# Feature-major products of a two-block layer: one 512-column moving operand instead of two of 256, and score products of two heads in turn

## The chip, the cores and the metric

The kernel runs on one core of a Trainium2 chip. The metric is device time in microseconds (us) of one execution. A core has five engines with queues of their own: TensorE (PE, matrix products; its weight loads are listed apart as PEld), VectorE (DVE), ScalarE (ACT), GpSimd (POOL) and SyncE (SP, which here only issues transfers). Each engine works its own list of instructions in order; semaphores tie them together.

## The reference

Two transformer blocks over 256 tokens of width 2048, in float32. Cut to what matters:

```python
# block 1                                    (h = rms_norm(x))
proj = h @ w_in                              # 2048 x 10752: q, k/v, DeltaNet q/k/v, gates
y = merge(nsa_mixer(...) @ w_up_nsa, gated_deltanet(...) @ w_up_dn)   # 1024 x 2048 each
x = x + y @ w_o
x = x + (silu(h2 @ w_ffn_gate) * (h2 @ w_ffn_up)) @ w_ffn_down        # D_FF = 5632
# block 2                                    (h = rms_norm_2(x))
proj = h @ w_in_2                            # RWKV-7 r, k, v, small parts, MLA latents
x = x + concat(rwkv7_mixer(...), mla_mixer(...)) @ w_out_2
gate = causal_conv3(h @ ffn_w_gate_2) + conv_b
x = x + (silu(gate) * (h @ ffn_w_up_2)) @ ffn_w_down_2
```

So nearly all work is matrix products with weights that are read once from memory.

## The kernel before

Float32 exactness is bought with a split: every weight chunk and every activation is written as a high part (fp32r, rounded) and a low part (the rest). A product is three: high x high, high x low, low x high (`mm3`).

Weights come through `wchunks`: SP loads a chunk of 1024 columns per partition (512 KB) into one of five `wraw` buffers, ACT rounds it to `whi` (three buffers), DVE subtracts to `wlo` (three buffers). `wsplit` gives these two instructions priority, so that they stand early in ACT's and DVE's lists.

There are two forms of product. Token-major ones (`gemm_tok`) hold activations as the stationary operand and stream 512 weight columns. Feature-major ones (`gemm_feat`) hold a 128x128 block of weights and stream the activations, 256 tokens. For every block of 128 output features and every k tile of 128 input features they run three products of 256 columns, each with its own weight load; `nm=4` blocks make a product group that fills one of the two `psA` accumulators (4 KB per partition, tile `mmA`). Consumers of a group are `merge_gate` and `merge_up` (gates of the two mixers), `Nsa.first` and `Nsa.q`, `DeltaNet.project` with `conv`, the gate and up loops of both feed-forward layers (FFN), and, with `nm=2`, `Rwkv.project`. A group is read out of the accumulator by one DVE instruction, in `Rwkv.project` by one ACT copy (`padded`).

The activations' parts are separate tiles in numbered slots: `sb`/`sc` and `sd`/`se` hold high and low part of the normed input, `hh`/`hl` that of the second FFN.

Around the mixers, generators are interleaved by `weave`: it always goes on with the first generator whose due time has come, by a table of costs in `Pace`, so that feature-major groups (bulk work) fill the gaps of the dependent chains (attention heads, DeltaNet and RWKV solves, small float32 products in the four `psB` accumulators, tile `pB`). `DeltaNet.project` puts finished groups in `raw` and stops when two are waiting. Outside of `weave` the work stands in program order.

RWKV's `solve` makes for each of four heads two score products (`bt`, `km` against `ar`) that use 64 of the 128 rows; MLA's `scores` makes for each of two heads a full product (`qn`, `kn`), one of 64 rows (`qr`, `kpe`) and a masking product.

Of the kernel before, what the change touches and what calls it, by code (L numbers as in the profile page):

```python
# [18 lines left out]
P = 128  # L19
# [183 lines left out]

class Kern:
    def __init__(self, tc, A, out, ctx):
# [9 lines left out]
        self.cst = None  # L215
        self.later = []

    def slot(self, which, shape, dt=F32):

        return (self.h2 if which in "bc" else self.hpool).tile(shape, dt, name="s" + which, tag="slot_" + which)  # L220
# [323 lines left out]
def hT_tiles(K, slots):  # L544
    return tuple(K.slot(s, [P, KD, T], F32R) for s in slots)


def hidden(K, pool, slots):

    return tuple(Cat(K.slot(s, [P, KD, T], F32R), pool.tile([P, KF - KD, T], F32R, name="hid" + n)) for s, n in zip(slots, "hl"))  # L550


def block1(K, ctx):
# [5 lines left out]
    H = hT_tiles(K, "bc")  # L559
# [22 lines left out]
    with ExitStack() as mix:  # L582
# [27 lines left out]
        M = hT_tiles(K, "bc")  # L610
        run(merge_up(K, dn.odn, A["w_up_dn"][0], td[0], tn, M))
    x = K.slot("a", [P, 2, D])
# [3 lines left out]
    H = hT_tiles(K, "de")  # L616
    run(add_proj(K, x, M, A["w_o"][0], KD, scale=0.5, after=norm_after(K, x, st, "norm2_w", H)))
    r = K.row_scale(st)
    with tc.tile_pool(name="ffn", bufs=1) as fp:
        hid = hidden(K, fp, "bc")  # L620
        for g in range(KF // 4):
            pg = run(K.gemm_feat(H, A["w_ffn_gate"][0], KD, 512 * g))
            if g == 0:
                rb = K.spread(r)
            sg = fp.tile([P, 4, T], F32, name="sg", bufs=2)
            rows4 = rb[:, None, :].to_broadcast([P, 4, T])
            nc.vector.tensor_tensor(sg, pg, rows4, op=ALU.mult)
            nc.scalar.activation(sg, sg, AF.Silu)
            nc.gpsimd.tensor_tensor(sg, sg, rows4, op=ALU.mult)
            pu = run(K.gemm_feat(H, A["w_ffn_up"][0], KD, 512 * g))  # L630
            nc.vector.tensor_tensor(sg, pu, sg, op=ALU.mult)
            K.split(sg, hid[0][:, 4 * g:4 * g + 4], hid[1][:, 4 * g:4 * g + 4])
# [5 lines left out]
        H = hT_tiles(K, "de")  # L638
# [48 lines left out]
def merge_gate(K, H, w_in, rb, half, dst):  # L687

    for g in range(4):
# [43 lines left out]
class DeltaNet:  # L733
# [59 lines left out]
    def conv(self, kind, grp):  # L793

        K, nc, pool = self.K, self.K.nc, self.pool
        while not self.raw:
            yield BLOCK
# [1030 lines left out]
```

## Time and profile before

| | before |
|---|---|
| median of three runs | 2831.42 us (2831.15 to 2832.09) |
| profiled execution | 2832.74 us, its span 2830.8 us |
| PE busy | 2795.0 us (99%), 20080 products |
| PEld busy | 2612.6 us (92%) |
| DVE busy | 1736.4 us (61%) |
| ACT busy | 1267.1 us (45%) |
| POOL busy | 209.8 us (7%) |
| granted TensorE clock | 0.996 of full speed |
| HBM read | 476.30 MB, 170 GB/s over the span |

The span is the time from the first to the last instruction of the profiled execution; 1.9 us of its own time lie around it. Busy shares are averages over very different stretches. The recorded end of a product is modelled and overlaps the next one, so the time that PE spends on one product is read from start to start of neighbours in the list, not from its duration.

### The profile page before, as it was taken

How to read it: one execution, taken by the hardware profiler on the slowest of the kernel's cores; microseconds unless marked ns; L12 is line 12 of the kernel's file. 1: busy time of each engine (PE TensorE's matmuls, PEld its weight loads, DVE VectorE, ACT ScalarE, POOL GpSimd, SP SyncE). 2: the span in 40 equal slices, each digit the busy share in tenths (PEclk: the TensorE clock that was granted, in tenths of full speed). 3: DMA queues.
4: the chain of work that ended last, by engine and by line, in shares of the span. 5: the costliest groups of instructions: out<-in, count | busy, mean ns of one | idle time of the engine just before them, and what ended most of it. 6: DMA issues, size and time to landing. Idle time of an engine off the chain costs nothing. (4 is left out here: it accounts for less than half of the span.)

```text
span 2830.8 us, 48442 instructions
## 1 busy us (share of the span) xinstructions
PE 2795.0 (99%) x20080; PEld 2612.6 (92%) x20080; DVE 1736.4 (61%) x2345; ACT 1267.1 (45%) x1582; POOL 209.8 (7%) x215
## 2 busy tenths in 40 slices
PE   9999999999999999999999999999999999999998
PEld 8997999999899999999888988878899999998888
DVE  6677758855555555555555687786576565655453
ACT  5446445444444444444444554545354444444443
POOL 0000100001000000000000322110000000000000
PEclk9999999999999999999999999999999999999999
DMA  7653366555666666666666653323566666665564
GB/s 234 207 153 115 98 172 180 162 145 183 225 183 180 186 180 186 183 183 188 197 198 186 198 152 98 108 72 123 185 176 181 185 181 184 181 185 189 194 194 138
DMA packets 285565, 484.68 MB, mean 171 GB/s; under 512 B 26113, under 2 KB 77057, under 8 KB 284706
## 3 DMA queue, kind: packets, MB, share of 16 engines
q1 hardware_dynamic: 282688, 475.94, 56.2%
q10 hardware_dynamic: 2658, 5.66, 0.6%
q8 instruction: 157, 2.57, 0.4%
q14 instruction: 62, 0.51, 0.0%
HBM read 476.30 MB, written 5.24 MB: 170 GB/s over the span
## 5 line engine op out<-in xcount | busy, mean ns | idle before, releaser
L257 DVE TENSOR_TENSOR wlo<-wraw,whi 128x1024 fp32r<-128x1024 f32 x889 | 1099.9, 1239 | 853.1 <-ACT whi L256 851.5
L256 ACT CAST whi<-wraw 128x1024 fp32r<-128x1024 f32 x889 | 928.2, 1045 | 1303.7 <-PE mmA L131 1237.6
L131 PE MATMUL mmA<-sd,whi 128*128 128x256 f32 x2256 | 605.4, 286 | 3.2 <-ACT sd L131 1.5
L131 PE MATMUL mmA<-sd,wlo 128*128 128x256 f32 x2048 | 582.1, 284 | 3.4 <-DVE wlo L257 3.4
L131 PE MATMUL mmA<-se,whi 128*128 128x256 f32 x2096 | 568.0, 284 | 0.0
L131 PEld LDWEIGHTS mmA<-sd,whi 128*128 128x128 f32 x2256 | 420.3, 193 | 5.3 <-ACT sd L131 1.7
L131 PE MATMUL mmA<-hh,whi 128*128 128x256 f32 x1408 | 398.7, 283 | 0.0
L131 PEld LDWEIGHTS mmA<-sd,wlo 128*128 128x128 f32 x2048 | 394.1, 192 | 4.9 <-DVE wlo L257 3.8
L131 PE MATMUL mmA<-hh,wlo 128*128 128x256 f32 x1408 | 398.5, 283 | 0.0
L131 PE MATMUL mmA<-hl,whi 128*128 128x256 f32 x1408 | 398.5, 283 | 0.0
L131 PEld LDWEIGHTS mmA<-se,whi 128*128 128x128 f32 x2096 | 393.6, 192 | 0.9 <-issue 0.7
L131 PE MATMUL mmA<-sb,whi 128*128 128x256 f32 x1152 | 331.8, 288 | 1.5 <-ACT whi L256 1.5
L131 PE MATMUL mmA<-sb,wlo 128*128 128x256 f32 x1152 | 328.2, 285 | 1.9 <-DVE wlo L257 1.9
L131 PE MATMUL mmA<-sc,whi 128*128 128x256 f32 x1152 | 327.7, 284 | 0.0
L131 PEld LDWEIGHTS mmA<-hl,whi 128*128 128x128 f32 x1408 | 270.3, 192 | 0.0
L131 PEld LDWEIGHTS mmA<-hh,whi 128*128 128x128 f32 x1408 | 270.3, 192 | 0.0
L131 PEld LDWEIGHTS mmA<-hh,wlo 128*128 128x128 f32 x1408 | 270.3, 192 | 0.0
L131 PEld LDWEIGHTS mmA<-sb,whi 128*128 128x128 f32 x1152 | 221.9, 193 | 3.0 <-ACT whi L256 1.7
L131 PEld LDWEIGHTS mmA<-sb,wlo 128*128 128x128 f32 x1152 | 221.9, 193 | 2.7 <-DVE wlo L257 2.3
L131 PEld LDWEIGHTS mmA<-sc,whi 128*128 128x128 f32 x1152 | 221.8, 193 | 0.9 <-issue 0.7
L131 PE MATMUL mmA<-whi,hidh 128*128 128x512 f32 (+1 forms) x504 | 184.2, 365 | 0.0
L131 PE MATMUL mmA<-wlo,hidh 128*128 128x512 f32 (+1 forms) x504 | 184.2, 365 | 0.0
(418 smaller groups left out, 3749.4 us busy)
## 6 DMA issues: line engine op xcount, KB each, us to landing
wraw<-in_w_in_dram SPq DMA_DIRECT2D x232, 512.0 KB, 3.7
wraw<-in_w_ffn_gate_dram SPq DMA_DIRECT2D x88, 512.0 KB, 3.8
wraw<-in_w_ffn_up_dram SPq DMA_DIRECT2D x88, 512.0 KB, 3.7
wraw<-in_w_ffn_down_dram SPq DMA_DIRECT2D x88, 512.0 KB, 4.7
wraw<-in_ffn_w_gate_dram SPq DMA_DIRECT2D x88, 512.0 KB, 3.7
wraw<-in_ffn_w_up_dram SPq DMA_DIRECT2D x88, 512.0 KB, 3.7
wraw<-in_ffn_w_down_dram SPq DMA_DIRECT2D x88, 512.0 KB, 4.6
wraw<-in_w_o_dram SPq DMA_DIRECT2D x32, 512.0 KB, 3.9
```

What stands on the lines that cost most here:

```text
L131: r = f(out, *a, **k)
L256: nc.nc.scalar.copy(h, r)
L257: nc.nc.vector.tensor_sub(l, r, h.bitcast(F32))
```

## The change

Feature-major groups now hold two blocks of 128 features (`nm=2`), and the two activation parts of a k tile lie side by side in one tile (`Parts`; `sbc`, `sde`, `hh`). High x high and high x low become one product of 512 columns with one weight load; low x high stays one of 256. The accumulator holds two sums per block, so each group is read out by `fold`: an ACT copy of the one sum, then a DVE addition of the other. Weight chunks of these products become 4 k tiles x 256 columns instead of 2 x 512. The slots move into pools of their own (`pair`, `new_side`). In `solve` and `scores` the products of two heads are written in turn.

```diff
+class Parts:
+    def __init__(self, both):
+        self.both = both
+    def __getitem__(self, i):
+        return self.both[:, :, i]
+    def wide(self, k):
+        return self.both[:, k].rearrange("p i t -> p (i t)")
...
-    def gemm_feat(self, X, W, kt, c0, nm=4, xk0=0, wk0=0):
-        ps = self.psA.tile([P, 4, T], F32, name="mmA")
+    def gemm_feat(self, X, W, kt, c0, nm=2, xk0=0, wk0=0):
+        ps = self.psA.tile([P, 2, 2, T], F32, name="mmA")
         for k, wh, wl in self.wchunks(W, kt, c0, nm * P, wk0):
-            for m in range(nm):
-                ms = slice(m * P, (m + 1) * P)
-                self.mm3(ps[:, m, :], (wh[:, ms], wl[:, ms]), [a[:, xk0 + k, :] for a in X],
-                         k == 0 and m % 2 == 0, k == kt - 1)
+            self.wide(ps, X, xk0 + k, wh, wl, range(nm), k == 0, k == kt - 1)
             yield FILL
         return ps
+    def wide(self, ps, X, k, wh, wl, blocks, start, stop):
+        for m in blocks:
+            ms = slice(m * P, (m + 1) * P)
+            self.mm(ps[:, m].rearrange("p i t -> p (i t)"), wh[:, ms], X.wide(k), start, stop)
+            self.mm(ps[:, m, 0], wl[:, ms], X[0][:, k], False, stop)
+    def fold(self, out, ps):
+        self.nc.scalar.copy(out, ps[:, :, 1])
+        self.nc.vector.tensor_tensor(out, ps[:, :, 0], out, op=ALU.add)
...
-        for g in range(KF // 4):
-            pg = run(K.gemm_feat(H, A["w_ffn_gate"][0], KD, 512 * g))
+        for g in range(KF // 2):
+            pg = run(K.gemm_feat(H, A["w_ffn_gate"][0], KD, 256 * g))
...
-            nc.vector.tensor_tensor(sg, pg, rows4, op=ALU.mult)
+            K.fold(sg, pg)
+            nc.vector.tensor_tensor(sg, sg, rows2, op=ALU.mult)
             nc.scalar.activation(sg, sg, AF.Silu)
...
-    for g in range(4):
-        ps = yield from K.gemm_feat(X, W, 8, 512 * g)
-        gs = slice(4 * g, 4 * g + 4)
-        nc.vector.scalar_tensor_tensor(gate[:, gs], gate[:, gs], 1.0, ps, op0=ALU.add, op1=ALU.mult)
+    for g in range(8):
+        ps = yield from K.gemm_feat(X, W, 8, 256 * g)
+        gs = slice(2 * g, 2 * g + 2)
+        up = K.npool.tile([P, 512], F32, name="xn", bufs=3).rearrange("p (m t) -> p m t", m=2)
+        K.fold(up, ps)
+        nc.vector.scalar_tensor_tensor(gate[:, gs], gate[:, gs], 1.0, up, op0=ALU.add, op1=ALU.mult)
...
+        for m in range(2):
+            pss = [K.pB().rearrange("p (k i) -> p k i", k=4) for i in range(2)]
+            for k, src in enumerate((bt, km)):
+                for i, ps in enumerate(pss):
+                    hp = slice(64 * i, 64 * i + 64)
+                    K.mm(ps[:, 2 * k:2 * k + 2], src[hp, m, ns], ar[hp, m, :, ns], k == 0, True)
...
         for i in range(2):
+            K.mm(S[i][:, :nk * P], qn[:, i, qs], kn[:, i, :nk * P], True, False)
+        for i in range(2):
             hp = slice(64 * i, 64 * i + 64)
-            K.mm(S[i][:, :nk * P], qn[:, i, qs], kn[:, i, :nk * P], True, False)
             K.mm(S[i][:, :nk * P], qr[hp, 0, qs], kpe[hp, :nk * P], False, False)
+        for i in range(2):
             K.mm(S[i][:, t * P:nk * P], self.identb, self.negb, False, True)
```

Three places show how instructions move. On PE, the first gate product of the first FFN, right behind the token-major product with `w_o`, before:

```order
L131 MATMUL mmA<-wlo,sb 128x512
L131 MATMUL mmA<-whi,sc 128x512
L131 MATMUL mmA<-sd,whi 128x256
L131 MATMUL mmA<-se,whi 128x256
L131 MATMUL mmA<-sd,wlo 128x256
```

and in the changed kernel:

```order
L131 MATMUL mmA<-whi,sbc 128x512 x2
L131 MATMUL mmA<-wlo,sbc 128x512
L131 MATMUL mmA<-whi,sbc 128x512
L131 MATMUL mmA<-sde,whi 128x512
L131 MATMUL mmA<-sde,wlo 128x256
```

The three products of 256 columns with `sd`, `se`, `sd` have become a pair with `sde`, 512 and 256 columns. Over the whole list 4544 such triples of 256 columns have become 4544 pairs; the other products with split weights keep shape and number.

On DVE, the last group of the second `merge_up` (`sd` is the gate, `sb`/`sc` or `sbc` the merged activation's parts), before:

```order
L257 TENSOR_TENSOR wlo<-wraw,whi 128x1024 x3
L131 SCALAR_TENSOR_TENSOR sd<-sd,mmA 128x1024
L257 TENSOR_TENSOR wlo<-wraw,whi 128x1024
L131 TENSOR_TENSOR sc<-sd,sb 128x1024
L257 TENSOR_TENSOR wlo<-wraw,whi 128x1024 x7
```

and in the changed kernel:

```order
L131 TENSOR_TENSOR xn<-mmA,xn 128x512
L131 SCALAR_TENSOR_TENSOR sd<-sd,xn 128x512
L282 TENSOR_TENSOR wlo<-wraw,whi 128x1024
L131 TENSOR_TENSOR sbc<-sd,sbc 128x2x256
L282 TENSOR_TENSOR wlo<-wraw,whi 128x1024 x6
```

Between two groups there stand now two weight subtractions instead of four, and a group of half the size has an addition (`xn<-mmA,xn`) more.

On PE, one call of MLA's `scores` for the second half of the tokens (the two `pB` accumulators are the two heads), before:

```order
L131 MATMUL pB_19862<-kn_19597,qn_19595 128x256
L131 MATMUL pB_19862<-kpe_15884,qr_19596 128x256
L131 LDWEIGHTS identb_15604
L131 MATMUL pB_19862<-negb_15605,identb_15604 128x128
L131 MATMUL pB_19863<-kn_19597,qn_19595 128x256
L131 MATMUL pB_19863<-kpe_15884,qr_19596 128x256
```

and in the changed kernel:

```order
L131 MATMUL pB_17145<-kn_16880,qn_16878 128x256
L131 MATMUL pB_17146<-kn_16880,qn_16878 128x256
L131 MATMUL pB_17145<-kpe_13535,qr_16879 128x256
L131 MATMUL pB_17146<-kpe_13535,qr_16879 128x256
L131 LDWEIGHTS identb_13255
L131 MATMUL pB_17145<-negb_13256,identb_13255 128x128
```

The two products of 64 rows now stand next to each other.

## Rows read from the trace of the kernel before

**Rows 1.** Windows view: stretch, its length, busy time (count) by engine, clock, DMA.

```profile
core 0: us, PE busy (x) PEld busy (x) DVE busy (x) ACT busy (x) POOL busy (x), PEclk, DMA share, GB/s
0.00:100.00 100.00, 93.69 (x771) 91.12 (x772) 65.75 (x108) 51.77 (x73) 4.56 (x10) 0.98 0.74 226
200.00:300.00 100.00, 99.83 (x585) 77.18 (x584) 77.49 (x147) 63.92 (x120) 0.82 (x6) 1.00 0.43 125
850.00:1290.00 440.00, 440.00 (x3669) 440.00 (x3669) 227.69 (x182) 180.11 (x172) 24.16 (x10) 1.00 0.63 184
1600.00:1670.00 70.00, 69.41 (x498) 64.04 (x497) 56.11 (x86) 32.19 (x41) 19.60 (x23) 1.00 0.53 151
1800.00:1900.00 100.00, 92.91 (x679) 82.04 (x678) 75.94 (x170) 45.98 (x88) 18.04 (x22) 0.98 0.26 76
```

**Rows 2.** Timeline of PE, first FFN, first and 85th row: start, duration, operation.

```profile
999.83 0.28 PE L131 MATMUL mmA<-sd,wlo 128*128 128x256 f32 x1
...
1009.91 0.28 PE L131 MATMUL mmA<-sd,wlo 128*128 128x256 f32 x1
```

**Rows 3.** Timeline of PE, token-major 512-column products, first and 40th row.

```profile
1755.08 0.40 PE L131 MATMUL mmA<-whi,se 128*128 128x512 f32 x1
...
1763.92 0.39 PE L131 MATMUL mmA<-whi,se 128*128 128x512 f32 x1
```

**Rows 4.** Timeline of PE where the two widths meet, both ways round.

```profile
277.25 0.39 PE L131 MATMUL mmA<-whi,sc 128*128 128x512 f32 x1
277.47 0.28 PE L131 MATMUL mmA<-sb,whi 128*128 128x256 f32 x1
...
477.08 0.28 PE L131 MATMUL mmA<-sb,wlo 128*128 128x256 f32 x1
477.20 0.40 PE L131 MATMUL mmA<-whi,sb 128*128 128x512 f32 x1
```

**Rows 5.** Groups by line and form: shapes, count, busy us, mean ns, idle before.

```profile
L256 ACT CAST whi<-wraw 128x1024 fp32r<-128x1024 f32 x872 | 914.2, 1049 | 1284.9 <-PE mmA L131 1224.0 <-issue 43.9 <-ACT sg L131 9.1
L257 DVE TENSOR_TENSOR wlo<-wraw,whi 128x1024 fp32r<-128x1024 f32 x872 | 1083.8, 1245 | 846.3 <-ACT whi L256 844.7
L131 ACT COPY psb<-mmA 128x512 f32<-128x512 f32 x13 | 7.6, 581 | 0.0
L131 DVE TENSOR_TENSOR cb<-mmA,rb 128x512 f32<-128x512 f32 x12 | 7.8, 687 | 3.4 <-PE mmA L131 3.4
```

**Rows 6.** Timeline of DVE in the second `merge_up`, idle time and releaser in brackets.

```profile
675.01 1.22 DVE L131 SCALAR_TENSOR_TENSOR sd<-sd,mmA 128x1024 f32<-128x1024 f32 x1 [0.69 <-PE mmA L131]
676.14 1.22 DVE L257 TENSOR_TENSOR wlo<-wraw,whi 128x1024 fp32r<-128x1024 f32 x1
680.74 1.22 DVE L131 TENSOR_TENSOR sc<-sd,sb 128x1024 fp32r<-128x1024 f32 x1 [3.37 <-ACT sb L131]
```

**Rows 7.** Timeline of POOL in the same place.

```profile
676.31 3.31 POOL L131 TENSOR_TENSOR sd<-sd,sa 128x1024 f32<-128x1024 f32 x1 [62.98 <-DVE sd L131]
```

**Rows 8.** DMA view of 1600 to 1670 us, then of 1000 to 1070 us.

```profile
DMA packets 8492, 10.55 MB, mean 151 GB/s; under 512 B 320, under 2 KB 6437, under 8 KB 8485
...
DMA packets 6607, 12.80 MB, mean 183 GB/s; under 512 B 384, under 2 KB 384, under 8 KB 6603
```

**Rows 9.** Timeline of PE in RWKV's first two solves, score products.

```profile
1644.04 0.71 PE L131 MATMUL pB<-ar,bt 64*128 64x256 f32 x4
1644.57 0.61 PE L131 MATMUL pB<-ar,km 64*128 64x256 f32 x4
...
1646.73 0.70 PE L131 MATMUL pB<-ar,bt 64*128 64x256 f32 x2 [0.59 <-DVE MM L131]
...
1649.09 0.59 PE L131 MATMUL pB<-ar,km 64*128 64x256 f32 x2
```

**Rows 10.** Timeline of PE in one call of MLA's `scores`, one head.

```profile
1888.70 0.70 PE L131 MATMUL pB<-kpe,qr 64*128 64x256 f32 x2
1889.33 0.23 PE L131 MATMUL pB<-negb,identb 128*128 128x128 bf16 x1
```

More of the change, by code (lines that the diff above doesn't have):

```diff
@@ L541, in __getitem__, with hidden @@
         return tile_[(p, slice(s.start - o, s.stop - o) if isinstance(k, slice) else k - o, *c)]
[L544 to L550, printed above, removed]
+def hidden(K, pool, heads):
+    return tuple(Cat(h, pool.tile([P, KF - KD, T], F32R, name="hid" + n)) for h, n in zip(heads, "hl"))
 def block1(K, ctx):
@@ L558, in block1 @@
     K.wake()
-    H = hT_tiles(K, "bc")
+    H = K.pair("bc")
     st = K.sums()
@@ L637, in block1 @@
         st = K.sums()
-        H = hT_tiles(K, "de")
+        H = K.pair("de")
         def after(g, t, xg):
@@ L787, in project @@
         for kind in (1, 0, 2):
-            while len(self.raw) > 1:
-                yield BLOCK
-            ps = yield from self.K.gemm_feat(self.H, self.w_in, KD, C_DN + 1024 * kind + 512 * grp)
-            self.raw.append(ps)
+            for hf in range(2):
+                while len(self.raw) > 1:
+                    yield BLOCK
+                ps = yield from self.K.gemm_feat(self.H, self.w_in, KD, C_DN + 1024 * kind + 512 * grp + 256 * hf)
+                self.raw.append(ps)
     def conv(self, kind, grp):
         K, nc, pool = self.K, self.K.nc, self.pool
-        while not self.raw:
-            yield BLOCK
-        ps = self.raw[0]
         out = pool.tile([P, 4, T], F32, name="cy", bufs=2)
         for hf in range(2):
+            while not self.raw:
+                yield BLOCK
+            ps = self.raw[0]
             cb = pool.tile([P, 2, T + 3], F32, name="cb", bufs=2)
             nc.gpsimd.memset(cb[:, :, 0:3], 0.0)
-            nc.vector.tensor_tensor(cb[:, :, 3:], ps[:, 2 * hf:2 * hf + 2], self.rb[:, None, :].to_broadcast([P, 2, T]), op=ALU.mult)
+            K.fold(cb[:, :, 3:], ps)
+            nc.vector.tensor_tensor(cb[:, :, 3:], cb[:, :, 3:], self.rb[:, None, :].to_broadcast([P, 2, T]), op=ALU.mult)
             th = pool.tile([P, 2, T], F32, name="th", bufs=2)
@@ L1000, in first @@
         K, nc = self.K, self.K.nc
+        raw = K.npool.tile([P, 512], F32, name="xn", bufs=3).rearrange("p (m t) -> p m t", m=2)
         ps = yield from K.gemm_feat(self.H, self.w_in, KD, C_KV)
+        K.fold(raw, ps)
+        ps = yield from K.gemm_feat(self.H, self.w_in, KD, C_KV + 256)
+        K.fold(self.raw[1], ps)
         K.load_mix(op, "sin")
@@ L1092, in q @@
     def q(self, hk):
-        ps = yield from self.K.gemm_feat(self.H, self.w_in, KD, C_Q + 512 * hk)
-        rope(self.K, self.pool, ps, 4, self.qT[:, 4 * hk:4 * hk + 4])
+        for h in range(4 * hk, 4 * hk + 4, 2):
+            ps = yield from self.K.gemm_feat(self.H, self.w_in, KD, C_Q + P * h)
+            q = self.K.npool.tile([P, 512], F32, name="xn", bufs=3).rearrange("p (m t) -> p m t", m=2)
+            self.K.fold(q, ps)
+            rope(self.K, self.pool, q, 2, self.qT[:, h:h + 2])
     def streams(self):
@@ L1259, in fill @@
                     yield BLOCK
+            K.new_side()
             M.load(R.cos2, R.sin2)
@@ L1455, in project @@
             ps = yield from K.gemm_feat(self.H, self.w_in, KD, 1024 * kind + 256 * q, nm=2)
-            raw.append((kind, self.padded(pp, ps[:, 0:2])))
+            raw.append((kind, self.padded(pp, ps, K.fold)))
             if len(raw) == 1:
```

103 lines of the change are left out of this document (56 added, 47 removed).

## Prediction

> **What bounds the kernel now.** I read the table of engines first: PE is busy for 2795.0 of 2830.8 us, DVE for 61%, ACT for 45%. A kernel like that gains by PE time alone, unless the change makes PE wait. The windows say where it waits now [rows 1]: never between 850 and 1290 us (first FFN: 3669 products in 440 us, 0.1199 each), 0.6 of 70 us in RWKV's stretch, 6.3 of the first 100 us and 7.1 of 100 us at 1800 (MLA), where small dependent steps run. PE's idle time is 2830.8 - 2795.0 = 35.8 us in all. PEld is busy as long as PE in the FFN, so loads keep up with products of 256 columns there.
>
> Next, what a product costs from start to start. In the FFN's timeline 84 steps take 10.08 us, 0.1200 each, for 256 columns [rows 2]; in a token-major stretch 39 steps take 8.84 us, 0.2267 each, for 512 [rows 3]. Twice 0.1200 is 0.2400, so two narrow products cost 13.3 ns more than one wide one. Read as a line, that is 0.1067 us per 256 columns and 13.3 ns for every product. Where the widths meet, the step follows the product that starts it: 0.22 after one of 512, 0.12 after one of 256 [rows 4]; no extra price of a mixture shows.
>
> **The pairs.** Before, a block and k tile cost 3 x 0.1200 = 0.3600 us; after, 0.2267 + 0.1200 = 0.3467. The change has 4544 of them: 34 groups of k = 16 in block 1 (C_KV 2, q 4, DeltaNet 12, gates 16), of 32 pairs each, 16 merge_up groups of 16, 88 FFN and 12 RWKV groups of 32: 1088 + 256 + 2816 + 384. 4544 x 13.3 ns = **-60.4 us**, on the path, since PE is the bound.
>
> The trace has no pair, so its weight load beside the 256-column product is not shown. Loads stood behind every 256-column product without idle time [rows 1, 2], and there are now two loads for 0.3467 us instead of three for 0.3600, so I add nothing. The upper bound is that nothing is saved: 0. The lower bound is 60.4 a little exceeded, by the rounding of the rows (0.01 us in 8.84 and 10.08, under 2 us in the sum).
>
> A rule speaks against this term. The Trainium skill, "TensorE: Matmul & The Clock Gate", section "Wait — 56ns, not 53.3ns?", gives each warm product its columns at 2.4 GHz and only 2.5 ns on top. By it, as an estimate, a triple takes 327.5 ns and a pair 325.0, and the change is worth 4544 x 2.5 = 11.4 us. The trace differs: 120.0 and 226.7 ns.
>
> **Products of 64 rows.** In MLA one head's product of 64 rows spans 1888.70 to 1889.33, where the masking product starts: 0.63 us for two passes of 256 columns [rows 10]. If the two heads' products, on different halves of the rows, run at the same time when they stand together, one of the two is saved: 0.63 in each of four calls at 256 columns, and in each of four at 128 between half of it and all, I take 0.4: 4 us. In RWKV heads already overlap before: four `bt` starts stand ahead of the first `km`, though the list has bt, km, bt, km by head [rows 9]. These four start within 0.53 us, 0.13 each, and at that pace a solve's 16 products take 2.1 us; the second solve's last from 1646.73 to 1649.68 (1649.09 + 0.59), 2.95 us. Bringing all eight solves from 2.95 to 2.1 would give 7 us. But a solve waits for DVE ahead of these products [rows 9], and six of the eight have their heads in turn after the change, two are still parted by other products: I take 2. Together **-6**, bounds 0 and -11.
>
> A rule bears on this too: the Trainium skill, "TensorE: Matmul & The Clock Gate", section "The mechanism" of Part 3, says that products start and end in strict order of the list, without reordering. By it no two heads' `bt` could run together with a `km` of the first between them, and the alternation would halve every solve: as an estimate 8 x 2.95 / 2 = 12 us and MLA's 4. The rows show starts out of the list's order.
>
> **The fold.** The 150 groups get an ACT copy (0.581 us for 128x512 out of the accumulator) and a DVE addition (0.687) [rows 5]: 87 us of ACT and 103 us of DVE. (Instructions on 1024 elements become two on 512: 2 x 0.69 against 1.22 [rows 5, 6], 0.16 us more, off the path like these.) ACT goes to 1267 + 87 = 1354 us, DVE to 1736 + 103 = 1839 of some 2770: no new bound by sum. On the path they count only where PE needs the accumulator or the result. There are two accumulators, and a group of 32 pairs lasts 32 x 0.3467 = 11.1 us; the weight casts and subtractions that stand ahead in ACT's and DVE's lists by priority (1.05 and 1.25 us [rows 5]) delay a fold by two or three of them, some 3.5 us, so it ends 7.6 us before the accumulator is wanted. Nor does DVE fall behind in the FFN, where a gate and an up group last 22.2 us: DVE has eight weight subtractions (10.0), two additions (1.4), two multiplications and a split (3 x 0.69 = 2.1) in them, 13.5 us, and in block 2 the convolution. So I add nothing; without that cover it would be (0.581 + 0.687) x 150 = 190 us.
>
> **merge_up.** The second one runs alone, with groups of 16 pairs, 5.55 us. Behind each group the old list has the multiplication by the gate (1.22), POOL's addition (3.31 [rows 7]) and the high/low split, the last at 680.74, 3.4 us late behind ACT [rows 6]. Now half sizes: a cast 1.05, a subtraction 1.25, addition 0.69, gate 0.69, POOL 1.66, ACT's cast 0.6: 5.9 us, against 5.55. The chain is no loop (next group's products need only the accumulator), so most of it is pipelined; I take **+2** for its end, where `w_o` waits for the last group's result; bounds 0 and +4 (a POOL addition and a cast more).
>
> **Start.** `Nsa.first` alternates its products with the four x groups. PE idles 6.3 us in this window [rows 1]; a group of half the blocks gives it 2.8 us of work (8 pairs) per x group, not 5.8, until its second half. **+2**, bounds 0 and +6 (the idle time doubled).
>
> **Woven stretches.** At 200 to 300 DVE is at 77% with PE at 99.8% [rows 1]; DVE gets a fold (0.69) every 11.1 us, 6% more, and reaches 84%. At 1800 to 1900 it is at 76% with PE idle 7.1 us, but no feature-major groups run there. `raw` holds two groups as before, now of 22 us of PE time instead of 46, so that `project` stops earlier while it waits for a solve. Idle time that is not at the start is 35.8 - 6.3 = 29.5 us. I take **+4**, and for the bound that it doubles, +30.
>
> **Transfers.** The new chunks have pieces of 1 KB, where old ones had 2 KB, at the same bytes. At 1600 to 1670, where `Rwkv.project` already reads such pieces (6437 of 8492 packets are under 2 KB), 151 GB/s take a share of 0.53, 0.0035 per GB/s; at 1000 to 1070 (384 under 2 KB of 6607) [rows 8] and over the FFN 184 GB/s take 0.63, 0.0034 [rows 1]. So the FFN's share becomes 0.63 x 0.0035 / 0.0034 = 0.65, and with 4% less time 0.67: hidden, nothing added. The new pools move slots, and I see no instruction whose wait they lengthen: nothing, with the bound in the +30.
>
> **Sum.** -60.4 - 6 + 2 + 2 + 4 = -58.4 against the profiled execution, 2832.74, gives 2774.3. The median is 1.3 us lower, so **2773.0 us** (2.1% less).
>
> **Rivals.**
> *Waits take a part of it back* (start and woven stretches two thirds of the way from the 6 us that I took to their bounds of 6 + 30): 20 us more, 2793. For it: DVE above 80% in chains that wait on it, half as much work in `raw`. Against: PE at 99.8% in that window has slack to lose little.
> *More than forecast*: the products of 64 rows give 12 us in RWKV (each solve halved, because `km` of one head did hold up the other's `bt`) and 4 in MLA, 10 more than I took, and half of the waits stay away (4 less): 2773 - 14 = 2759. For it: one solve of 2.95 us is well above the other's pace; against: four `bt` starts in 0.53 us ahead of any `km` [rows 9], and DVE ends the waits there. (This is the case that the skill's rule of strict order stands for.)
> *The saving is not per product*: what 256 columns cost over their share of 512 is something of the stretch [rows 2] (loads at their limit, PEld 100% busy there) that two loads per 0.3467 us still pay. With no saving, 2773 + 60 = 2833, unchanged. (With the skill's 2.5 ns instead, the estimate is 2773 + 60.4 - 11.4 = 2822.) As a mechanism of this kernel: a pair would then take 0.36 us, or a little less. Against: the steps of rows 2 and 4 agree on 0.12 wherever the product stands.
> *Slower*: PE waits at each group's end for the fold. It decides from 60.4 / 150 = 0.40 us per group on; one weight cast more ahead of the copy that frees the accumulator would be 1.05 us if nothing covered it. At 0.6 us, 90 us: 2773 + 90 = 2863. Against: the 7.6 us of cover worked out above; for it: in `merge_up` the cover is only 5.55 - 3.5 = 2 us.
>
> **How the numbers follow.** The forecast within -11 and +12 (2762 to 2785): 0.65. Waits that take back 20: 0.16. More: 0.09. Not per product: 0.05, of which 0.03 within 0.2% of before (5.7 us, about what a measurement of this kernel can tell from no change). Slower: 0.04, as no mistake of a single term reaches it; remaining cases 0.01 lie among the faster. Faster is then 0.65 + 0.16 + 0.09 + 0.02 + 0.01 = 0.93, same 0.03, slower 0.04. The range 2758 to 2800 holds the first three but for a tail, and leaves out about 0.13.
>
> **What the profile after would show.** Right: in the FFN a pair every 0.3467 us (32 pairs in 11.1 us), PE busy 100%, about 15540 products (4544 fewer), span some 58 us shorter, 37.5 of it (2816 x 13.3 ns) in the two FFN's gate and up products; ACT about 1354 and DVE 1839 us. In MLA's calls two `kpe` products of 256 columns in the time of one. Wrong: 0.36 us per pair (the load is not hidden); PE idle time behind `xn` or `sg` at group ends; PE idle over 60 us in all, named behind DVE in the woven stretches; DMA as releaser of weight casts in the FFN.

## The result, and the profile after

The changed kernel takes 2804.14 us (2801.37 to 2805.63, four runs) against 2831.76 (2831.15 to 2834.38, four runs) for the kernel before in the same comparison: a ratio of 0.99, interval 0.9882 to 0.9917. It is 1% faster. The forecast was 2773 with a range of 2758 to 2800: the direction was right, 28 us came instead of 58, and the time lies 4 us above the range.

The table of engines of the changed kernel (busy us, share of the span, instructions):

```profile
PE 2757.7 (98%) x15536; PEld 2366.9 (84%) x15536; DVE 1840.3 (66%) x2587; ACT 1336.1 (48%) x1776; POOL 226.8 (8%) x254
```

4544 products fewer, as counted, and DVE where the sum had put it (1839). But PE's idle time went from 35.8 to 2803.8 - 2757.7 = 46.1 us, and PE's busy time fell by 37 us, not 60.

Where the time went is seen when both executions are cut at the same places of the program. The windows view of the kernel before, with the columns of [rows 1]; the seven stages are: block 1 up to the product with `w_o`, that product, the first FFN's gate and up products, its down projection, block 2's mixers up to the second FFN, that one's gate and up products, the rest.

```profile
0.00:709.37 709.37, 700.40 (x5429) 664.34 (x5430) 486.79 (x757) 352.11 (x487) 38.30 (x50) 0.99 0.56 165
709.37:799.23 89.86, 89.86 (x411) 74.51 (x409) 51.80 (x58) 42.59 (x53) 3.30 (x1) 1.00 0.67 216
799.23:1307.39 508.16, 508.16 (x4237) 508.16 (x4236) 265.01 (x219) 210.24 (x205) 26.57 (x11) 1.00 0.63 183
1307.39:1550.46 243.07, 242.80 (x1082) 200.60 (x1081) 124.89 (x120) 101.59 (x113) 9.25 (x6) 1.00 0.62 194
1550.46:2067.16 516.70, 502.30 (x3373) 444.72 (x3372) 374.44 (x718) 251.72 (x412) 88.31 (x116) 0.99 0.45 135
2067.16:2575.64 508.48, 508.46 (x4239) 508.26 (x4238) 312.57 (x359) 210.23 (x210) 28.36 (x21) 1.00 0.63 182
2575.64:2830.80 255.16, 243.06 (x1322) 211.96 (x1320) 120.86 (x115) 98.66 (x104) 15.74 (x10) 0.98 0.55 178
```

The same stages of the changed kernel:

```profile
0.00:692.52 692.52, 683.85 (x4085) 587.84 (x4085) 525.61 (x831) 376.96 (x548) 39.76 (x56) 1.00 0.55 170
692.52:782.34 89.82, 89.82 (x410) 74.57 (x409) 53.54 (x61) 42.88 (x55) 1.29 (x1) 1.00 0.62 212
782.34:1278.00 495.66, 495.66 (x2830) 434.56 (x2829) 288.53 (x295) 231.74 (x270) 39.16 (x22) 1.00 0.59 187
1278.00:1521.07 243.07, 242.80 (x1082) 200.61 (x1081) 124.40 (x121) 101.51 (x114) 9.23 (x6) 1.00 0.59 194
1521.07:2050.15 529.08, 502.61 (x2990) 424.37 (x2988) 382.24 (x730) 251.91 (x412) 90.92 (x117) 0.98 0.42 132
2050.15:2548.95 498.80, 498.80 (x2832) 432.75 (x2831) 345.33 (x435) 232.48 (x275) 30.73 (x42) 1.00 0.58 185
2548.95:2803.80 254.85, 244.14 (x1322) 212.22 (x1320) 120.61 (x117) 98.58 (x105) 15.73 (x10) 0.99 0.52 178
```

Block 1 gained 16.9 us, the two FFNs 12.5 and 9.7 (18.7 each were forecast), the stages that the change leaves alone moved by 0.3 at most in sum, and block 2's mixers, which were to gain, lost 12.4. So two things are to be explained: the FFNs, where PE never idles and yet little more than half of the gain came, and the mixers' stage.

The FFN's pairs by the timeline, where [rows 2] showed 0.1200 us a product. First FFN, first and 63rd row (31 pairs):

```profile
999.80 0.28 PE L131 MATMUL mmA<-sde,wlo 128*128 128x256 f32 x1
...
1010.68 0.28 PE L131 MATMUL mmA<-sde,wlo 128*128 128x256 f32 x1
...
2199.74 0.28 PE L131 MATMUL mmA<-hh,wlo 128*128 128x256 f32 x1
...
2210.69 0.28 PE L131 MATMUL mmA<-hh,wlo 128*128 128x256 f32 x1
```

The last two rows are the second FFN's, 31 pairs apart as well. A pair takes 10.88 / 31 = 0.3510 us in the first and 10.95 / 31 = 0.3532 in the second, where 0.3467 was worked out.

### The profile page after: what moved, and what is told of

Its sections match the earlier page's. It is cut to its first block, busy times and chain, and to the rows that moved or that the text cites. A ratio compares the mean times of both kernels' runs of the same rounds, so it can differ in the third digit from the quotient of the medians.

```text
span 2803.8 us, 39866 instructions
## 1 busy us (share of the span) xinstructions
PE 2757.7 (98%) x15536; PEld 2366.9 (84%) x15536; DVE 1840.3 (66%) x2587; ACT 1336.1 (48%) x1776; POOL 226.8 (8%) x254
## 4 chain that ended last, share of the span: by engine, by line
PE 93%; DVE 4%; issue 1%; DMA 1%; POOL 1%; ACT 1%; ACTq 0%; DVEq 0%; SPq 0%; POOLq 0%
PE mmA L131 83%; PE pB L131 9%; DVE wlo L282 1%; DVE iw L131 0%; DVE xn L131 0%; DVE sd L131 0%; DMA cst<-in_consts_dram 0%; ACT whi L281 0%; DVE MM L131 0%; DMA dn_nrm<-in_dn_norm_w_dram 0%; DVE tmp L131 0%; POOL sa L131 0%; DVE bt L131 0%; DMA wraw<-in_mla_w_ukv_dram 0%; POOL psb L131 0%
## 5 line engine op out<-in xcount | busy, mean ns | idle before, releaser
L131 PE MATMUL mmA<-sde,whi 128*128 128x512 f32 (+1 forms) x1888 | 652.8, 390 | 5.4 <-DVE iw L131 3.0
L131 PE MATMUL mmA<-sde,wlo 128*128 128x256 f32 x1840 | 523.0, 284 | 1.0 <-DVE wlo L282 1.0
L131 PE MATMUL mmA<-hh,whi 128*128 128x512 f32 x1408 | 497.6, 399 | 0.0
L131 PEld LDWEIGHTS mmA<-sde,whi 128*128 128x128 f32 x1888 | 352.7, 188 | 83.1 <-issue 3.4
L131 PE MATMUL mmA<-sbc,whi 128*128 128x512 f32 (+1 forms) x1216 | 413.6, 388 | 2.7 <-DVE sbc L131 2.7
L131 PEld LDWEIGHTS mmA<-sde,wlo 128*128 128x128 f32 x1840 | 347.1, 189 | 2.7 <-DVE wlo L282 1.5
L131 PE MATMUL mmA<-sbc,wlo 128*128 128x256 f32 x1152 | 324.7, 282 | 1.8 <-DVE wlo L282 1.8
L131 PEld LDWEIGHTS mmA<-sbc,whi 128*128 128x128 f32 x1216 | 225.0, 189 | 50.3 <-ACT whi L281 2.9
L131 PE MATMUL mmA<-whi,sbc 128*128 128x512 f32 (+1 forms) x768 | 231.2, 375 | 0.0
L131 PEld LDWEIGHTS mmA<-sbc,wlo 128*128 128x128 f32 x1152 | 218.5, 190 | 3.2 <-DVE wlo L282 2.2
```

The lines of the kernel that those rows point to most:

```text
L131: r = f(out, *a, **k)
```

## The experiments

All times of stages below are lengths of windows cut at the first product of the stage and of the next, so they are read beside the two tables above. They come from one profiled execution each; block 1's stage differs by some 2 us either way between executions of like kernels, the FFN's by 0.2.

### The order of wide and narrow products

```diff
 e1_grouped: for each weight chunk (4 k tiles x 2 blocks)
-    wide(m0) narrow(m0) wide(m1) narrow(m1), k tile by k tile
+    eight wide products, then the eight narrow ones
```

> The changed kernel, with the products of a weight chunk grouped by width: eight of 512 columns, then eight of 256, in place of 512 and 256 in turn. Theory (the alternation of widths costs 4.5 to 6.7 ns per pair): a pair falls from 352 to 353 ns to about 347, gate and up of the first FFN from 495.7 to 488 us and of the second from 498.7 to 488 us, the whole by some 20 to 26 us to about 2780. Rival (a wide product of this kind costs 232 instead of 227 ns whatever stands beside it): both FFNs unchanged. The mixer's stage in block 2 (529 us) moves by less than 5 us by both, unless its order changes by chance.

Measured: 2793.58 us (ratio to before 0.9865, 0.9848 to 0.9881). First FFN, then second FFN (the mixers' stage took 524.8 us):

```profile
781.33:1277.21 495.88, 495.88 (x2829) 432.99 (x2828) 288.15 (x295) 232.96 (x271) 39.11 (x22) 1.00 0.59 187
2045.11:2538.32 493.21, 493.21 (x2831) 433.78 (x2830) 343.84 (x435) 234.41 (x276) 30.57 (x42) 1.00 0.59 187
```

The first FFN did not move (495.9), the second gained 5.6 us. Neither theory holds by itself: if changing the width were the whole price, both had to come to 488, with an eighth of the changes left; if it cost nothing, the second could not have gained.

```diff
 e2_skewed
-    wide(m0) narrow(m0) wide(m1) narrow(m1)
+    wide(m0,k) wide(m1,k) narrow(m0,k) wide(m0,k+1) narrow(m1,k) ...
```

> The changed kernel, with the widths still in turn, but each product of 256 columns written behind the next wide one, so that it adds into another block's part of the accumulator than the product just before it. Theory (alternation of widths): a pair stays at 351 to 353 ns, FFN stages 495 to 499 us. Rival (the narrow product pays because it adds to columns that the wide one has just written): a pair falls to 347 ns and each FFN stage to 488 us.

Measured: 2805.90 us, FFN stages 496.4 and 497.8. The rival falls, which wanted 488 in both: that the narrow product adds to columns just written is worth 1 us of a stage at most (498.8 against 497.8 in the second FFN).

```diff
 e6_order_forms
+first FFN:  wide(m0) wide(m1) narrow(m0) narrow(m1), k tile by k tile
+second FFN: mm(ps[:, m, 0], wh, hi); mm(ps[:, m, 1], wh, lo); mm(ps[:, m, 0], wl, hi)
```

> The changed kernel; in the first FFN the two wide products of a k tile come first, then its two narrow ones; in the second FFN every pair is written as the old three products of 256 columns, still into two sums with the fold. First FFN: 351 to 352 ns a pair (495 us) if any mixture costs the same, 347 (488 us) if only the change from block to block did. Second FFN: 0.360 us a triple, 507 us, if groups of two blocks and the fold cost nothing there; the rival, a wait at each of the 44 group ends, would put 10 us or more on top.

```profile
782.08:1273.93 491.85, 491.85 (x2829) 430.67 (x2828) 288.62 (x295) 231.64 (x271) 39.08 (x22) 1.00 0.59 189
2049.90:2558.39 508.49, 508.47 (x4240) 508.27 (x4239) 340.34 (x435) 234.72 (x275) 36.08 (x42) 1.00 0.58 182
```

Two wide and two narrow in turn: 491.85 / 1408 = 0.3493 us a pair, better than either other order tried. This is the stage by its pairs, other products included; on the same measure the pairs one by one take 0.3520 (first FFN) and 0.3543 (second), some 1 ns more than from start to start. The timeline of the first FFN by k tile, a first row and the one 30 pairs behind it:

```profile
1000.14 0.62 PE L131 MATMUL mmA<-sde,whi 128*128 128x512 f32 x2
...
1010.59 0.62 PE L131 MATMUL mmA<-sde,whi 128*128 128x512 f32 x2
```

10.45 / 30 = 0.3483 us a pair, 1.6 ns above 0.3467. And the second FFN with triples, small groups and the fold takes 508.49 us, as before (508.48): groups of two blocks and 44 folds cost an FFN nothing.

### Wide products alone

To see which product pays, the FFNs ran 512-column products alone (outputs then lack or add terms, as the expectations say).

```diff
 e5_wide_forms
+first FFN:  mm(both sums of m, wh, hi|lo)                                  # no narrow product
+second FFN: mm(both sums of m, wh, hi|lo); mm(both sums of m, wl, hi|lo)
 e11_wide_swapped: the two forms exchanged between the FFNs
```

> The changed kernel; the first FFN's gate and up products leave the 256-column product (low x high) out, the second FFN's replace it by one of 512 columns (low x both parts), so both run 512-column products alone. Theory (products of 512 columns step at 226.7 ns as long as no product of 256 columns is near): 226 to 227 ns from start to start in both, gate and up in 1408 x 0.2267 = 319 us in the first FFN and 638 us in the second. Rival (a wide product with the weights as the stationary operand costs 231 to 237 ns by itself): 325 to 334 us and 650 to 667 us.

> The forms of the wide-product run swapped: the first FFN replaces the 256-column product by one of 512 (low x both parts), the second leaves it out. Theory (the form decides, 227 ns where a bank gets two wide products in a row and 232 where banks alternate at every product): first FFN 639 us, second 328 us. Rival (the place decides, that is the tiles and addresses of each FFN): first FFN 654 us, second 319 us.

The first FFN of e5 (1408 products) took 328.8 us, as the rival had it, and the second (2816) came out as the theory had it:

```profile
1880.85:2520.81 639.96, 639.96 (x2831) 530.27 (x2830) 345.57 (x435) 232.77 (x275) 30.73 (x42) 1.00 0.46 144
```

The first FFN of e11 (2816 products):

```profile
780.58:1436.31 655.73, 655.73 (x2830) 531.78 (x2828) 288.56 (x295) 231.79 (x271) 39.16 (x22) 1.00 0.45 141
```

With the same form, low x both added, the first FFN takes 655.7 / 2816 = 0.2329 us a product and the second 640.0 / 2816 = 0.2273: the place decides, not the form. (e11's second FFN, 342.5 us for 1408 products, can't be divided so: PE idles 14.7 us there, 11.8 of them behind weight casts.) e12 took two more forms, each high x both product twice in a row in the first FFN (so low x high is missing and high x both counts twice), and both blocks' products with high, then with low weights in the second:

> The changed kernel with 512-column products alone in both FFNs: the first runs each high x both product twice in a row, the second runs high x both for both blocks, then low x both for both blocks. Theory (accumulator banks that change at every product cost some 5 ns): first FFN 227 ns a step, 639 us; second 232 ns, 654 us. Rival (what counts is that weights come from the high and the low tile in turn): first FFN 232 ns, 654 us; second between 227 and 232.

655.7 and 640.0 us once more. The theory on accumulator banks falls. The rival falls with e11, whose first FFN takes high and low weights in turn and steps at 0.2329 all the same.

### The start of the operands

What differs between the FFNs is where the tiles start. The compiled programs put them at these byte addresses of a partition (the remainder within 512 in brackets):

```
                  whi, wlo    sb..se, hh of before   sde          hh
before            all (96)    all (96)               -            120928 (96)
changed kernel    all (96)    -                      196576 (480) 88160 (96)
```

`sde` lies in the new pool `side`, which is placed from the end of memory, and starts 384 bytes off the rest, counted within 512; `sd` and `se`, where the changed kernel still uses them, lie there too (480), `sa` and `sbc` at 96. e13 swaps the starts by unused tiles of 384 bytes and runs low x both as well:

```diff
 e13_swap_places
+        if which == "de":
+            self.side.tile([P, 96], F32, name="pad")       # sde at 96
...
+        fp.tile([P, 96], F32, name="pad")                  # hh at 480
         H = Parts(fp.tile([P, KD, 2, T], F32R, name="hh"))
```

> 512-column products alone in both FFNs (high x both, low x both), with small unused tiles put beside the activations so that their starts within 512 bytes are swapped: 96 in the first FFN (as all weights), 480 in the second, whose hidden activations move to 480 as well. Theory (the start of an operand relative to the other's sets the step): first FFN 227 ns, 639 us; second 232 ns, 654 us; the second down projection, where the hidden activations are the stationary operand, 232 instead of 227 ns a product. Rival (something else of the first FFN's place): 654 us and 639 us as without the swap.

The timeline of PE: first FFN, first and 46th row, then second FFN, first and 44th row, then second down projection (hidden activations stationary), first and 40th row:

```profile
999.77 0.39 PE L131 MATMUL mmA<-sde,wlo 128*128 128x512 f32 x1
...
1009.97 0.39 PE L131 MATMUL mmA<-sde,whi 128*128 128x512 f32 x1
...
2299.81 0.40 PE L131 MATMUL mmA<-hh,whi 128*128 128x512 f32 x1
...
2309.80 0.40 PE L131 MATMUL mmA<-hh,wlo 128*128 128x512 f32 x1
...
2879.73 0.39 PE L131 MATMUL mmA<-wlo,hidh 128*128 128x512 f32 x1
...
2888.80 0.39 PE L131 MATMUL mmA<-wlo,hidh 128*128 128x512 f32 x1
```

10.20 / 45 = 0.2267 us where the start is now 96, 9.99 / 43 = 0.2323 where it is 480, and 9.07 / 39 = 0.2326 in the down projection, where products of this kind had 0.2267 [rows 3]. The price moved with the start, on the stationary side too. e17 moved the weights instead:

```diff
 e17_weights_moved
+        self.cpool.tile([P, 96], F32, name="pad")          # whi, wlo at 480; sde stays at 480
+        fp.tile([P, 32], F32, name="pad")                  # hh at 96
```

> 512-column products alone in both FFNs (high x both, low x both). The weights' tiles now start at 480 within 512 bytes, the first FFN's activations at 480 too, the second's at 96. Theory (the difference of the two starts sets the step): first FFN 227 ns, 639.7 us; second 232 ns, 655.8 us. Rival (the activations' start by itself does): first 655.7 us, second 640 us, as without the move.

```profile
779.45:1419.12 639.67, 639.67 (x2830) 529.98 (x2828) 288.42 (x295) 232.17 (x271) 39.14 (x22) 1.00 0.47 145
2191.26:2847.17 655.91, 655.91 (x2831) 531.67 (x2830) 345.15 (x435) 232.70 (x275) 30.50 (x42) 1.00 0.45 141
```

Equal starts 0.2272 us a product, unequal 0.2329: it is the difference of the two operands' starts, not the place of one. Products of 256 columns don't show it: with triples alone (e8, below) the first FFN takes 508.2 us with `sde` at 480, the second 508.5 with `hh` at 96.

The changed kernel itself pays some of this price in a stage that the change was to leave alone. The last third of its second down projection holds `sa` (96) and `se` (480) against weights at 96; first and 46th row:

```profile
2609.23 0.39 PE L131 MATMUL mmA<-whi,sa 128*128 128x512 f32 x1
...
2619.63 0.39 PE L131 MATMUL mmA<-whi,sa 128*128 128x512 f32 x1
```

10.40 / 45 = 0.2311 us, where the kernel before, with all starts at 96, takes 10.20 us for the same 45 steps (2635.51 to 2645.71), 0.2267. Over the 288 products of this kind that is 1.3 us, and PE's busy time in the last stage did rise from 243.1 to 244.1 us; less idle time hides it in the stage's length. Only every third product there, `whi` with `se`, has unequal starts, yet the mean rose by 4.4 ns, three quarters of the 5.9 or so that a stream of unequal starts pays: how far one such product slows its neighbours is not shown.

Then the same with the changed kernel's own pairs:

```diff
 e15_swapped_pairs: pairs, sde at 96, hh at 480
 e16_other_places:  pairs, sde at 224, hh at 352
```

> The changed kernel with its pairs, and the two FFNs' starts swapped as for the wide products. Theory (a pair's time goes with the start): first FFN 353.4 ns a pair (498 us), second 351.2 (495.5 us), each that of the other before. Rival (it goes with the FFN): 495.7 and 498.7 us as in the changed kernel.

> The changed kernel with its pairs, the first FFN's activations started at 224 and the second's at 352 within 512 bytes. If some start frees the mixture of its price, one of the stages falls to 488 to 490 us (347 to 348 ns a pair); if a mixture always costs 4 to 7 ns, both stay at 494 to 500 us.

```profile
781.18:1279.81 498.63, 498.63 (x2829) 432.64 (x2828) 288.53 (x295) 231.82 (x270) 39.19 (x22) 1.00 0.60 186
2048.87:2544.68 495.81, 495.81 (x2832) 434.61 (x2831) 344.53 (x435) 232.44 (x275) 30.52 (x42) 1.00 0.59 186
```

These are e15's: the FFNs exchanged their times. e16 gave 495.7 (at 224) and 498.8 us (at 352). So a pair in turn takes 2 ns less where the starts differ by 384 or 128 than where they are equal, and where they differ by 256 (e16's second FFN) it takes as long as at equal ones; all are 4 to 7 ns above 346.7: with equal starts the whole price is the mixture's, since wide products alone step at 0.2267 there. What in the mixture costs it stays open: not the number of changes of width alone (e1, with an eighth of them, takes longer than e6 and e10 with half), not the columns just written (e2), and no start tried frees it (e15, e16).

### The scores

```diff
 e3_old_scores: the changed kernel, scores as in the kernel before
 e4_new_scores: the kernel before, scores as in the changed kernel
```

> The changed kernel with the score products of RWKV and MLA written in the old order. Theory (the mixer stage of block 2, 529 us against 517 before, lost its time because bulk products and chains stand in another order and the fold delays the chains; the score order saves 3 to 6 us): the stage takes 530 to 535 us, the whole 2807 to 2810. Rival (the new order of the scores, which parts a head's products and holds two accumulators at once, makes the loss): the stage takes 508 to 514 us, the whole about 2787.

> The kernel before with only the score products of two heads in turn. Theory (scores save 3 to 6 us): the mixer stage of block 2 takes 511 to 514 us instead of 517, the whole 2826 to 2829. Rival (the new order costs waits): the stage takes 525 to 530 us, the whole 2840 to 2845.

2807.46 and 2831.96 us; the mixers' stage 529.9 (529.1 with the new order) and 517.6 (516.7 with the old). The order of the scores moves the stage by less than 1 us, and once for the better and once for the worse; the whole kernels differ by 3.3 us (2804.14 and 2807.46) and 0.9 (2831.07, the kernel before beside e4, and 2831.96), about what executions of one kernel differ by (2801.37 to 2805.63). In MLA the products did what was forecast. Two heads at 256 columns, and behind them a whole RWKV solve, in the timeline of the changed kernel:

```profile
1875.18 0.70 PE L131 MATMUL pB<-kpe,qr 64*128 64x256 f32 x4
1875.82 0.28 PE L131 MATMUL pB<-negb,identb 128*128 128x128 bf16 x2
...
1878.01 0.70 PE L131 MATMUL pB<-ar,bt 64*128 64x256 f32 x4
...
1879.41 0.60 PE L131 MATMUL pB<-ar,km 64*128 64x256 f32 x4
```

Two heads take 0.64 us where one took 0.63 [rows 10], and the solve's 16 products 2.0 us (1878.01 to 1880.01) where 2.1 was worked out from [rows 9]. But in RWKV that is hardly a gain. The first solve of the kernel before starts at 1644.04 [rows 9], and its last score products are these, so that it took 2.10 us in the old order:

```profile
1645.44 0.70 PE L131 MATMUL pB<-ar,km 64*128 64x256 f32 x4
```

And the changed kernel's second solve, with its heads in turn, lasts from 1641.30 to 1644.24, 2.94 us, as the one of 2.95 before:

```profile
1641.30 1.08 PE L131 MATMUL pB<-ar,bt 64*128 64x256 f32 x3
...
1643.44 0.80 PE L131 MATMUL pB<-ar,km 64*128 64x256 f32 x3
```

What PE does save turns into waiting, as far as one execution each shows. With the new order its busy time in the stage falls from 505.9 (e3) to 502.6 us and its idle time rises from 24.0 to 26.5; in the kernel before, 502.3 falls to 501.4 (e4) and 14.4 rises to 16.2.

### The mixers' stage of block 2

```diff
 e8_all_triples: every pair written as three products into the same two sums
 e7_rwkv_old
-            ps = yield from K.gemm_feat(self.H, self.w_in, KD, 1024 * kind + 256 * q, nm=2)
-            raw.append((kind, self.padded(pp, ps, K.fold)))
+            ps = yield from K.gemm_old(self.H, self.w_in, KD, 1024 * kind + 256 * q)
+            raw.append((kind, self.padded(pp, ps[:, 0:2], K.nc.scalar.copy)))
 e9_unplanned: as the changed kernel, RWKV's fold with
-        self.nc.vector.tensor_tensor(out, ps[:, :, 0], out, op=ALU.add)
+        self.nc.nc.vector.tensor_tensor(out, ps[:, :, 0], out, op=ALU.add)   # past Pace's count
```

> The changed kernel with every wide pair written as three products of 256 columns into the same two sums: groups of two blocks, fold, 1 KB pieces and pools stay, only the wide product is undone. Theory (these parts cost some 10 to 20 us in the woven stages and nothing in the FFNs): 2840 to 2850. Rival (they cost nothing, and the loss in block 2's mixer comes from the pairs themselves): 2831 as before, mixer stage 517.

> The changed kernel with RWKV's twelve projection groups as before (three products of 256 columns, one sum, one ACT copy, no fold); all else is the change's. Theory (the fold's DVE addition queues behind weight subtractions and delays RWKV's chains): block 2's mixer stage falls from 529 us to 515 to 520, the whole to about 2793. Rival (another thing in this stage, the order of the woven list or the pools, makes it): the stage stays at 527 to 535 us, the whole 2803 to 2810.

> The changed kernel; only the table of costs that orders the woven lists is not charged for the fold's DVE addition in RWKV's projections, so that the lists stand nearly as where RWKV keeps its old groups, while the addition itself is still done. Theory (the loss in block 2's mixer is the order of the lists that the charge brings about): the stage takes 514 to 519 us instead of 529, the whole about 2793. Rival (the addition really makes the chains' data late): 525 to 531 us, the whole 2801 to 2807.

e8: 2837.13 us (ratio 1.0022, 1.0013 to 1.0031). Its block 1 and its mixers:

```profile
0.00:703.39 703.39, 695.25 (x5428) 659.55 (x5429) 525.33 (x831) 377.53 (x548) 38.00 (x56) 1.00 0.54 167
...
1544.38:2070.82 526.44, 501.61 (x3374) 441.52 (x3372) 379.64 (x730) 251.18 (x412) 89.32 (x117) 0.99 0.43 133
```

Without any wide product the mixers lose 9.7 us already, and block 1 gains 6.0. e7, 2792.46 us (ratio 0.9861), and e9, 2792.74 us (0.9863), in the mixers' stage:

```profile
1520.99:2037.49 516.50, 499.84 (x3373) 441.34 (x3372) 374.46 (x718) 251.96 (x412) 90.38 (x117) 0.99 0.43 136
```

```profile
1519.42:2036.69 517.27, 498.48 (x2990) 422.24 (x2988) 377.99 (x730) 251.89 (x412) 90.61 (x117) 0.99 0.43 135
```

e9 does every fold, on the same engines with the same data, and is as fast as e7 without them, to 0.8 us. (Its pairs save PE 1.4 us of busy time there and its idle time is 2.1 us longer than e7's, 18.8 against 16.7, so the folds may cost some 2 us there, not 12.) So the fold itself is not what makes the stage late; its charge in the table of costs is, by the order that `weave` then writes. One place of it is PE's list between the two `blk64` products (`pB<-tmp,cst`) of the last `prepare`, the chain of small products ahead of a solve. In the changed kernel three bulk products (`mmA`) stand there:

```
L131 MATMUL pB<-tmp,cst 128x512
L131 MATMUL pB<-sh,wB 128x256 x2
L131 MATMUL pB<-ident,bon 128x128 x4
L131 MATMUL pB<-ident,Xo_15812 128x128 x2
L131 MATMUL pB<-X_15758,Lo_15760 128x128 x2
L131 MATMUL mmA<-whi,sd 128x256
L131 MATMUL mmA<-wlo,sd 128x256
L131 MATMUL mmA<-whi,sd 128x256
L131 MATMUL pB<-Y_15975,XT_15849 128x128 x2
L131 MATMUL pB<-tmp,cst 128x512
```

in e9's list there are 29 of them between the same two. The timeline of the changed kernel at that place (idle time and its releaser in brackets):

```profile
1842.30 0.71 PE L131 MATMUL pB<-Y,XT 128*128 128x128 f32 x4 [1.51 <-ACT bt L131]
1847.66 2.04 PE L131 MATMUL pB<-tmp,cst 128*128 128x512 f32 x2 [4.65 <-DVE tmp L131]
```

and of e9:

```profile
1836.17 1.10 PE L131 MATMUL pB<-tmp,cst 128*128 128x512 f32 x2 [1.94 <-DVE tmp L131]
```

The bulk products had been used up ahead of the chain. Over the stage PE idles 26.5 us (529.08 - 502.61) in the changed kernel and 18.8 in e9. The other 4 us of the difference are busy time (502.6 against 498.5), and the granted clock goes with them. The windows of 30 us around this place and of the following ones up to the product with `w_out`, changed kernel and then e9:

```profile
1830.00:1860.00 30.00, 19.27 (x114) 15.38 (x112) 20.79 (x40) 10.92 (x20) 8.36 (x10) 0.86 0.24 75
1860.00:1924.80 64.80, 63.03 (x483) 57.61 (x483) 51.59 (x136) 32.84 (x65) 3.88 (x8) 0.96 0.23 76
```

```profile
1828.35:1858.35 30.00, 24.54 (x166) 21.95 (x165) 19.96 (x37) 13.36 (x27) 6.62 (x9) 0.89 0.13 42
1858.35:1911.45 53.10, 51.84 (x409) 46.68 (x407) 46.78 (x122) 29.25 (x56) 2.72 (x6) 1.00 0.29 93
```

Where PE had idled 10.7 of 30 us, the granted clock is 0.86 and still 0.96 in the next stretch, means between its full 2.4 and its lower 1.2 GHz; where it had idled 5.5 us, it is 0.89 and then 1.00.

### Versions that beat both

```diff
 e10_by_tile: e7, and all pairs as wide(m0) wide(m1) narrow(m0) narrow(m1)
 e14_aligned_by_tile: e10, and sde at 96
 e18_fold_unplanned: e10, and no fold charged to the table of costs anywhere
```

> RWKV's projection groups as before (no fold there), and all other pairs with the two wide products of a k tile first, then the two narrow ones. Theory (order by k tile gives 348 to 349 ns a pair wherever it runs): first FFN 491.7 us, second 492 to 494 instead of 498.7, block 2's mixer 516 to 518, the whole 2780 to 2785. Rival (the step depends on the place, not on this order): second FFN 498 us, the whole 2787 to 2790.

> The kernel with RWKV's old groups and the order by k tile (2783.8 us), and the first FFN's activations started at 96 within 512 bytes. Theory (the start sets the wide product's step and the mixture costs on top of it): by k tile the second FFN, which has that start already, takes 491.9 us, so the first stays at 491 to 492 and the whole at 2782 to 2785. Rival (the two prices add up): first FFN 484 us, the whole 2776.

> The kernel with RWKV's old groups and the order by k tile (2783.8 us), with no fold charged to the table of costs that orders the woven lists, in block 1 either. Theory (block 1's 6 us, too, are a matter of the order that the charge brings about): block 1 up to the product with w_o takes some 699 us instead of 693.7, the whole 2787 to 2790. Rival (the gain comes from the smaller groups or the pools): 693 to 695 us, the whole 2783 to 2785.

e10: 2783.77 us (2783.12 to 2784.44), ratio to before 0.9833 (0.9817 to 0.985), with e14 the best of all. Its mixers' stage takes 516.3 us; its first FFN and second FFN:

```profile
783.53:1275.36 491.83, 491.83 (x2829) 430.64 (x2828) 288.62 (x295) 231.69 (x271) 39.08 (x22) 1.00 0.60 189
2034.73:2526.78 492.05, 492.05 (x2832) 429.20 (x2831) 343.93 (x435) 232.89 (x275) 30.88 (x42) 1.00 0.59 188
```

e14 took 2784.52 us (ratio 0.9831), its first FFN 491.8: by k tile a pair takes 0.3493 us of the stage at either start. e18 took 2786.27; its block 1 took 697.3 us against 693.7 in e10, between the two expectations. So some 3.6 of the 6 us that block 1 gained in e8 seem to go with the order too, from one execution each where 2 us are noise (the whole kernels differ by 2.5); the rest stays open.

## Why the prediction was wrong, step by step

- **The bound** was right: PE is busy for 98% of the span after, and each FFN came out as PE's time.
- **The pairs, -60.4 us: mis-sized.** The step that failed is "no extra price of a mixture shows". It rested on one row each way round, in steps of 0.01 us, while the price is 4 to 7 ns a pair. Measured, the FFNs' 2816 pairs gave 12.5 + 9.7 = 22.2 us, 7.9 ns a pair, not 13.3; block 1's 1344 gave 703.39 - 692.52 = 10.9 (e8 against the change), 8.1 ns; RWKV's 384 gave nothing at the end (e9 against e7). In the second FFN all of the miss is the mixture. In the first, wide products alone pay 5.7 ns for the new pool's start (655.7 against 639.7 us for 2816, e11 and e13), but pairs do not: given the start of the second FFN they took 3 us more (e15). So the new pool's start is no cause of the miss there. "I see no instruction whose wait they lengthen" was said of the new pools; what they changed was no wait but a step, to the cost of 1.3 us in the second down projection. The bound that was named, a pair at 0.36 us because a load isn't hidden, did not come: 0.351 and 0.353. The Trainium skill, "TensorE: Matmul & The Clock Gate", section "Wait — 56ns, not 53.3ns?", gives 2.5 ns on top of the columns. The traces show 13.3 in a uniform stream of equal starts, and a pair's gain of 7 to 9 ns lies between what the two would give.
- **The scores, -6 us: nothing came.** For MLA the mechanism was right on PE (0.64 us for two heads). For RWKV it was not: the solve of 2.95 us was taken for all eight, but the first one already took 2.10 us in the old order, and the second still takes 2.94 in the new. The stage moved by less than 1 us (e3, e4), since PE then waits longer for the chains. The reason against stood in the text ("a solve waits for DVE ahead of these products"); it cut RWKV's share from 7 us to 2, and MLA's not at all.
- **The fold, 0, was right**: 508.5 us in e6's second FFN, 508.2 in e8's first, as before, and in the mixers e9 against e7 (some 2 us of idle time at most). DVE's 1839 became 1840.3; ACT's 1354 became 1336.1, of which some 7 us are the twelve RWKV groups that had a copy before.
- **merge_up +2 and start +2: not seen.** Block 1 with groups of two blocks and the fold alone was 6.0 us faster, not slower (e8); the first 100 us idle 6.7 us (6.3 before), and PE is busy for all of the 24 us from 676 to 700, around the end of the second `merge_up`.
- **The woven stretches, +4: the sign was right, place and size were not.** This is the second step that failed. Rival one had 20 us more, and the mixers' stage lost 12.4 us where 5 of pairs and 6 of scores were to be won. Its reasons were not the ones named. DVE did reach 85% at 200 to 300 us (84 was worked out), but PE lost 0.3 us there, and `raw` belongs to block 1, which gained. The stretch at 1800 to 1900 was set aside because "no feature-major groups run there"; what hit it was the order of the lists in block 2, which moves when the planner is charged for one more instruction (e9: -11.8 us in the stage with the charge alone taken away). No term of the sum stood for that.
- **Transfers** were hidden, as said, and better than said: in the first FFN the share is 0.59 at 187 GB/s, not 0.67.

The sum by what was measured: pairs -10.9 in block 1 and -22.2 in the FFNs, block 1's other parts -6.0, the mixers +12.4, the rest -0.3, together -27.0; the spans differ by 2830.8 - 2803.8 = 27.0.

## What to carry to other kernels

A saving of a few nanoseconds in each of thousands of instructions must be read from long stretches of the very mixture that the change makes; where the trace has none, the two pure streams bound it only from one side. A list written by a planner with costs is an input of its own: an added instruction that is well hidden can still move its order, and taking the charge away while leaving the instruction in tells the two apart at once. When tiles move to another pool, look at where they start: the step of 512-column products can change with it.

## What the runs showed of the hardware

512-column products with 4-byte operands step at 0.2267 us when the moving and the stationary operand start at the same byte address within 512, and at 0.2323 to 0.2329 when the starts differ by 384, whichever of the two is moved (e13, e17); 256-column products took the same time at both (e8). Differences of 128 and 256 were tried with pairs alone, where 128 did as 384 and 256 as none, so that a period of 256 bytes would fit these runs as well as one of 512. And a mixture of 512 and 256 columns costs more than its parts, 0.348 (two and two, e6) to 0.353 us a pair instead of 0.3467, by an amount that goes with the order and, in turn, with the starts; why is open.
